# Block sums of the second channel weights: made by GpSimd, in other loop units, in a hybrid encoder layer

## The chip, the cores and the metric

The kernel runs on one core of one Trainium2 chip. The metric is device time in microseconds (us), the median of a few runs; lower is better. The core's engines are TensorE (PE, matmuls), VectorE (DVE), ScalarE (ACT), GpSimd (POOL) and SyncE (SP); before the change, every DMA is issued by SyncE.

## What is computed

One layer of a streaming encoder on x of 2048 tokens x 1024 channels, float32: a token mixer of four head groups (convolution, state-space scan, windowed attention, gated recurrence), and then the channel mixer, with which this case deals:

```python
h = rmsnorm(x, norm_ffn[l])
x = x + (jnp.square(jax.nn.relu(h @ w_ff1[l])) @ w_ff2[l]).astype(x.dtype)
```

w_ff1 is 1024 x 4096, w_ff2 4096 x 1024.

## The kernel before

The whole layer is one program. A scheduler turns the code into one fixed instruction order for each engine before the kernel runs: it goes by priorities (a block under `hi_()` has a high one), by data dependences and by the times that it assumes for every operation. Tiles come from pools; a tag has a fixed number of buffers, and whoever takes a buffer again waits for its last users. Each engine then works through its own order and waits where a semaphore has not come yet. SyncE too: a DMA that it cannot issue yet holds up all DMAs behind it.

Every float32 operand of a matmul is split into a rounded part and a rest (h and l, made by ScalarE and VectorE), and a product takes three passes: h.h, h.l, l.h.

**The channel mixer's products** are done by a scheme of seven block products instead of eight (Strassen's, in Winograd's form) at 2 x 2 blocks. It needs sums of blocks of both operands, and so there are four steps:

- `prep_step`: loads normed token rows (tile fxs), transposes them and makes the seven token operands. For the first token half they stay in SBUF; for the second they are stored to DRAM (tb) during units 2, 5, 8 and 11, and `from_dram` loads them again (tile tr, lines 1216 to 1218) when the second half begins.
- `ff1`: one unit makes 256 hidden channels for 1024 tokens: seven products of 12 matmuls (line 1267), relu and square on ScalarE (1273, 1274), block sums on VectorE (1138), and seven stores (as, line 1310). There are 16 units for each token half, 32 in all, here numbered 0 to 31 (n = 16 hf + j). ScalarE's copy at line 1286 stands once in each.
- `w_units`: loads four 128 x 512 blocks of w_ff1 for the next unit (a11, a12, a21, a22; tile wr, line 1134, six buffers), makes four sums on VectorE (the first adds a21 and a22) and splits seven operands (wh on ScalarE at line 1128, wl on VectorE at 1129).
- `w2_sums(k)`, k from 0 to 15: loads two rows of blocks of w_ff2, each 128 x 1024, 512 KB (x and y, tile w2r), forms four differences of 128 x 512 blocks in place, and stores both to DRAM (tt). The second phase of the mixer loads tt (`t_unit`) as the weight operand of four of its seven block products, after the units.

The second phase runs 7 x 8 groups of 48 matmuls (line 1397). Its token operands come back from DRAM through tile sr (`s_tile`, lines 1367 to 1369).

**What sets the order around the change.** fxs, tr, w2r and sr all take the tag xt, which has two buffers, in the order in which the code asks for them. Before the change that is: fxs of the fourth prep_step (unit 11), tr (14 loads), w2r (32 tiles, in units 16 to 31), sr. SyncE issues the loads and stores of w2_sums between the stores as and the loads wr of the units; VectorE makes the differences between the units' own sums.

Of the kernel before, what the change touches and what calls it, by code (L numbers as in the profile page):

```python
# [16 lines left out]
ALU = mybir.AluOpType  # L17
# [4 lines left out]
P = 128  # L22
# [37 lines left out]
def emit(ctx, tc, a):  # L60
    nc = tc.nc
    V, S, G, PE, SY = nc.vector, nc.scalar, nc.gpsimd, nc.tensor, nc.sync
# [104 lines left out]
    for r in range(2):  # L167
        SY.dma_start(out=sink[r * 64:(r + 1) * 64, :],
                     in_=a["attn_sinks"].rearrange("(k r) -> r k", r=2)[r].partition_broadcast(64),
# [945 lines left out]
    NJ = DFF // (2 * P)  # L1115
    as_d = [[dram.tile([P, 4, NJ, P], F32, name=f"as{i}_{h}") for h in range(2)] for i in range(7)]
    tt_d = [dram.tile([NJ, P, D], F32, name=f"tt{i}") for i in range(2)]
# [19 lines left out]
    def tsub(o, x, y, op=ALU.subtract):  # L1137
        V.tensor_tensor(out=o, in0=x, in1=y, op=op)  # L1138
# [15 lines left out]
    def prep_step(hf, i, put, tmp):  # L1154
        def trans(ps, xs, half):
            for k in range(4):
                kk = half * 4 + k
                PE.transpose(ps[:, k * P:(k + 1) * P], xs[:, kk * P:(kk + 1) * P], ident)

        o = i * P  # L1160
        xs = []
        for tb in range(2):
            x_ = big.tile([P, D], F32, tag="xt", name="fxs", bufs=2)
            SY.dma_start(out=x_, in_=x1_d[hf * 2 + tb][o:o + P, :])
            ss = c1.tile([P, 1], F32, tag="fss", name="fss", bufs=2)
            S.activation(out=junk, in_=x_, func=AF.Square, accum_out=ss)
            r = rstd_of(c1, ss, 1, 1.0 / D, "frs")
            V.scalar_tensor_tensor(out=x_, in0=x_, scalar=r, in1=g_ffn, op0=ALU.mult, op1=ALU.mult)
            xs.append(x_)
        p11, p22 = psum_tr(), psum_sx()  # L1170
        trans(p11, xs[0], 0)
        trans(p22, xs[1], 1)
        s11, s22 = tmp(), tmp()
        S.activation(out=s11, in_=p11, func=AF.Copy)
        S.activation(out=s22, in_=p22, func=AF.Copy)
        p12, p21 = psum_tr(), psum_sx()
        trans(p12, xs[1], 0)
        trans(p21, xs[0], 1)
        put(0, o, s11)
        put(1, o, p21)  # L1180
        t1, t2 = tmp(), tmp()
        tsub(t1, p12, s11)
        tsub(t2, s22, t1)
        t4 = tmp()
        tsub(t4, p21, t2)
        t3 = tmp()
        tsub(t3, s22, p12)
        put(2, o, t2)
        put(3, o, t1)
        put(4, o, t3)  # L1190
        put(5, o, s22)
        put(6, o, t4)
# [8 lines left out]
    def put_dram(tmp):  # L1201
        def put(i, o, src):
            if i == 1:
                c_ = tmp()
                S.activation(out=c_, in_=src, func=AF.Copy)
                src = c_
            SY.dma_start(out=tb_d[i][:, :, o:o + P], in_=src.rearrange("p (k t) -> p k t", k=4))
        return put

    def from_dram():  # L1210
        ops = operands()
        for i in range(7):
            for h in range(2):
                ks = slice(h * 2, h * 2 + 2)
                r = big.tile([P, 2, TB], F32, tag="xt", name="tr", bufs=2)
                SY.dma_start(out=r, in_=tb_d[i][:, ks, :])
                S.activation(out=ops[i][0][:, ks], in_=r, func=AF.Copy)
                V.tensor_tensor(out=ops[i][1][:, ks], in0=r, in1=ops[i][0][:, ks], op=ALU.subtract)
        return ops


    def w2_sums(k):
        x_, y_ = (big.tile([P, D], F32, tag="xt", name="w2r", bufs=2) for _ in range(2))
        for h, t_ in enumerate((x_, y_)):
            SY.dma_start(out=t_, in_=a["w_ff2"][(2 * k + h) * P:(2 * k + h + 1) * P, :])
        b11, b12, b21, b22 = x_[:, 0:512], x_[:, 512:], y_[:, 0:512], y_[:, 512:]
        tsub(b11, b12, b11)
        tsub(b12, b22, b12)
        tsub(b22, b22, b11)
        tsub(b21, b21, b22)  # L1230
        for h, t_ in enumerate((x_, y_)):
            SY.dma_start(out=tt_d[h][k], in_=t_)

    def w2(k, half, nd):
        return a["w_ff2"][(2 * k + half) * P:(2 * k + half + 1) * P, nd * 512:(nd + 1) * 512]
# [2 lines left out]
    def w_units(j, tmp):  # L1238
        f0 = j * 2 * P

        def raw(kh, fh):
            return raw512(a["w_ff1"][kh * 512:(kh + 1) * 512, f0 + fh * P:f0 + (fh + 1) * P]
                          .rearrange("(k p) c -> p k c", p=P))

        with hi_():
            a11, a12, a21, a22 = raw(0, 0), raw(1, 0), raw(0, 1), raw(1, 1)
            u = [split(a11), split(a12)]
            s1, s2 = tmp(), tmp()
            tsub(s1, a21, a22, ALU.add)
            tsub(s2, s1, a11)  # L1250
            u.append(split(s2))
            u.append(split(s1))
            s3, s4 = tmp(), tmp()
            tsub(s3, a11, a21)
            u.append(split(s3))
            tsub(s4, a12, s2)
            u.append(split(s4))
            u.append(split(a22))
        return u
# [16 lines left out]
    def ff1(hf, j, u, b, tmp):  # L1276
        pa, pb, pc = psum_mm(), psum_mx(), psum_hx()
        prod(pa, u[0], b[0], True)
        x1 = tmp()
        S.activation(out=x1, in_=pa, func=AF.Copy)  # L1280
        prod(pb, u[1], b[1], True)
        c11 = tmp()
        tsub(c11, pb, x1, ALU.add)
        prod(pa, u[2], b[2], False)
        u2 = tmp()
        S.activation(out=u2, in_=pa, func=AF.Copy)  # L1286
        relu2(c11, c11)
        prod(pc, u[3], b[3], True)
        p5 = tmp()
        S.activation(out=p5, in_=pc, func=AF.Copy)  # L1290
        prod(pa, u[4], b[4], False)
        c22 = tmp()
        tsub(c22, pa, p5, ALU.add)
        relu2(c22, c22)
        prod(pc, u[5], b[5], False)
        c12 = tmp()
        tsub(c12, pc, u2, ALU.add)
        relu2(c12, c12)
        prod(pa, u[6], b[6], False)
        c21 = tmp()  # L1300
        relu2(c21, pa)

        e11, e12, e21, e22 = c11, c21, c12, c22
        s1, s2, s3, s4 = tmp(), tmp(), tmp(), tmp()
        tsub(s1, e21, e22, ALU.add)
        tsub(s2, s1, e11)
        tsub(s3, e11, e21)
        tsub(s4, e12, s2)
        for i, t_ in enumerate((e11, e12, s2, s3, e22, s1, s4)):
            SY.dma_start(out=as_d[i][hf][:, :, j, :], in_=t_.rearrange("p (q t) -> p q t", q=4))  # L1310
# [9 lines left out]
    for hf in range(2):  # L1320
        for j in range(NJ):
            u = nxt
            if (hf, j) != (1, NJ - 1):
                nxt = w_units((j + 1) % NJ, tmp1)
            if hf == 0 and j in (2, 5, 8, 11):
                prep_step(1, (2, 5, 8, 11).index(j), put_dram(tmp1), tmp1)
            if hf == 1 and j == 0:
                with hi_():
                    b = from_dram()
            if hf == 1:  # L1330
                w2_sums(j)
            ff1(hf, j, u, b, tmp1)
    f2.close()

# [106 lines left out]
```

## Time and profile before

| what | value |
|---|---|
| median of 3 runs | 2346.17 us (2341.35 to 2346.51) |
| the profiled execution's own time | 2343.7 us |
| its span in the profile | 2341.6 us |
| TensorE matmul, busy | 2227.5 us (95%) |
| VectorE, busy | 1433.2 us (61%) |
| ScalarE, busy | 949.8 us (41%) |
| GpSimd, busy | 163.2 us (7%), 208 instructions |
| mean granted TensorE clock | 0.987 |

The span is the profiled execution from its first to its last instruction; its own time lies 2.1 us above. In the views, a row of the timeline is: start, duration, engine, line, operation, output <- inputs, shapes, count, and in brackets the engine's idle time ahead of it and what ended that. A row of waits is: engine, tile and line, what it waited for, total us, times, longest. A row of the table by stretch has the stretch, its length, then busy time and instruction count of each engine, the granted clock, the DMA engines' busy share and GB/s. A row of DMA issues gives the count, the size and the median time from issue to landing. PEld is TensorE's weight load.

### The profile page before, as it was taken

To read this page: it belongs to the slowest core of one execution; us is meant where nothing else is said; L and a number is where in the kernel's file an instruction comes from. 1 tells how busy PE (TensorE), PEld (TensorE's weight loads), DVE (VectorE), ACT (ScalarE), POOL (GpSimd) and SP (SyncE) were. 2 spreads that over 40 slices of the span, in tenths; PEclk is the share of its full clock that TensorE was granted. 3 is DMA by queue.
4 is the path that set the end of the run, shared out by engine and by line. 5 is a ranking of instruction groups with operands and counts; after the bars stand their busy time and mean duration, and the time that the engine had idled before them with its cause. 6 is when DMAs were issued, how large, how long until landed. Compare 5 with 4: busy or idle time off the path is not lost.

```text
span 2341.6 us, 32446 instructions
## 1 busy us (share of the span) xinstructions
PE 2227.5 (95%) x11460; PEld 1761.9 (75%) x11460; DVE 1433.2 (61%) x3008; ACT 949.8 (41%) x1902; POOL 163.2 (7%) x208
## 2 busy tenths in 40 slices
PE   7799999999999999989999999999999999999999
PEld 6577777777777777767777777777778888888887
DVE  5786786787677654676655666676653344344342
ACT  4234325435433433455555554544543233133121
POOL 0122212121211110000000000000000000000000
PEclk9899999999999999999999999999999999999999
DMA  6323333434432547636656577888674454355542
GB/s 182 92 78 97 104 102 118 118 101 125 124 111 85 163 155 224 216 129 193 194 158 191 173 222 255 273 266 267 204 238 151 155 192 140 118 190 180 183 148 99
DMA packets 393347, 381.35 MB, mean 163 GB/s; under 512 B 35968, under 2 KB 310496, under 8 KB 393184
## 3 DMA queue, kind: packets, MB, share of 16 engines
q1 hardware_dynamic: 393184, 379.27, 52.5%
q8 instruction: 90, 1.47, 0.3%
q14 instruction: 73, 0.60, 0.1%
HBM read 261.77 MB, written 116.40 MB: 161 GB/s over the span
## 4 chain that ended last, share of the span: by engine, by line
PE 67%; DVE 13%; DMA 9%; ACT 4%; issue 3%; POOL 2%; SPq 1%; DVEq 0%; POOLq 0%; ACTq 0%
PE mm L1397 26%; PE mm L1267 10%; PE mm L509 5%; PE mm L511 5%; PE mm L510 5%; PE hx L1267 5%; DMA w2r<-in_w_ff_dram 2%; DVE wl L111 2%; PE mx L1267 2%; DVE tp L1138 2%; PE hx L921 1%; DMA fxs<-x1d 1%; PE mx L826 1%; ACT wh L1128 1%; DVE w2r L1138 1%
## 5 line engine op out<-in xcount | busy, mean ns | idle before, releaser
L1397 PE MATMUL mm<-wh,st 128*128 128x512 f32 x1792 | 561.8, 394 | 1.4 <-ACT wh L1128 1.4
L1397 PEld LDWEIGHTS mm<-wh,st 128*128 128x128 f32 x1792 | 337.4, 188 | 80.0 <-ACT wh L1128 1.9
L1397 PE MATMUL mm<-wl,st 128*128 128x512 f32 x896 | 353.6, 395 | 0.2 <-DVE wl L1129 0.2
L1267 PE MATMUL mm<-tb,wh 128*128 128x512 f32 x1024 | 330.3, 403 | 24.5 <-ACT tp L1280 6.5
L1368 ACT ACTIVATE st<-sr 128x1024 fp32r<-128x1024 f32 x112 | 114.6, 1054 | 402.8 <-PE mm L1397 359.2
L1267 PEld LDWEIGHTS mm<-tb,wh 128*128 128x128 f32 x1024 | 189.6, 191 | 85.1 <-ACT tp L1286 14.7
L105 ACT ACTIVATE wh<-wr 128x512 fp32r<-128x512 f32 x224 | 138.6, 628 | 201.8 <-PE mm L510 163.0
L509 PE MATMUL mm<-wh,hh 128*128 128x512 f32 x512 | 208.3, 407 | 2.1 <-ACT hh L504 2.1
L1129 DVE TENSOR_TENSOR wl<-wr,wh 128x512 fp32r<-128x512 f32 x208 | 138.1, 688 | 113.6 <-ACT wh L1128 70.2
L1267 PE MATMUL mm<-tb,wl 128*128 128x512 f32 x512 | 204.5, 399 | 0.0
L511 PE MATMUL mm<-wh,hl 128*128 128x512 f32 x512 | 204.4, 399 | 0.0
L510 PE MATMUL mm<-wl,hh 128*128 128x512 f32 x512 | 204.0, 398 | 0.0
L1397 PEld LDWEIGHTS mm<-wl,st 128*128 128x128 f32 x896 | 168.4, 188 | 40.5 <-DVE wl L1129 0.5
L1369 DVE TENSOR_TENSOR st<-sr,st 128x1024 fp32r<-128x1024 f32 x112 | 133.9, 1222 | 94.8 <-ACT st L1368 94.6
L1267 PE MATMUL hx<-tb,wh 128*128 128x512 f32 x512 | 162.3, 397 | 8.4 <-ACT wh L1128 8.4
L111 DVE TENSOR_TENSOR wl<-wr,wh 128x512 fp32r<-128x512 f32 x224 | 151.3, 694 | 30.5 <-ACT wh L105 26.3
L509 PE MATMUL mm<-hh,wh 128*128 128x512 f32 x384 | 159.5, 415 | 0.0
L511 PE MATMUL mm<-hh,wl 128*128 128x512 f32 x384 | 154.9, 403 | 0.0
L510 PE MATMUL mm<-hl,wh 128*128 128x512 f32 x384 | 154.5, 402 | 0.0
L1128 ACT ACTIVATE wh<-wr 128x512 fp32r<-128x512 f32 x208 | 125.4, 625 | 64.6 <-PE mm L1267 28.1
L1138 DVE TENSOR_TENSOR tq<-mm,tq 128x512 f32<-128x512 f32 x32 | 22.1, 691 | 173.0 <-PE mm L1397 172.9
L1273 ACT ACTIVATE tp<-tp 128x512 f32<-128x512 f32 x96 | 60.5, 630 | 163.0 <-DVE tp L1138 156.2
(372 smaller groups left out, 3627.6 us busy)
## 6 DMA issues: line engine op xcount, KB each, us to landing
as<-tp SPq DMA_DIRECT2D x224, 256.0 KB, 2.8
sr<-as SPq DMA_DIRECT2D x112, 512.0 KB, 4.4
wr<-in_w_ff_dram SPq DMA_DIRECT2D x176, 256.0 KB, 3.8
wr<-in_w_in_dram SPq DMA_DIRECT2D x160, 256.0 KB, 3.1
wr<-in_w_out_dram SPq DMA_DIRECT2D x64, 256.0 KB, 4.1
w2r<-in_w_ff_dram SPq DMA_DIRECT2D x32, 512.0 KB, 4.6
tt<-w2r SPq DMA_DIRECT2D x32, 512.0 KB, 2.7
wr<-tt SPq DMA_DIRECT2D x64, 256.0 KB, 4.0
```

The source lines that it names most:

```text
L105: S.activation(out=hi, in_=raw, func=AF.Copy)
L111: (G if le == "p" else V).tensor_tensor(out=lo, in0=raw, in1=hi, op=ALU.subtract)
L509: PE.matmul(ps, lhsT=lh, rhs=rh, start=first, stop=False)
L510: PE.matmul(ps, lhsT=lh, rhs=rl, start=False, stop=False)
L511: PE.matmul(ps, lhsT=ll, rhs=rh, start=False, stop=last)
L1128: S.activation(out=h, in_=raw, func=AF.Copy)
L1129: V.tensor_tensor(out=l, in0=raw, in1=h, op=ALU.subtract)
L1138: V.tensor_tensor(out=o, in0=x, in1=y, op=op)
L1267: PE.matmul(ps, lhsT=(wh, wl)[lw][:, ks], rhs=b[lb][:, k, :], start=first and k == 0 and q == 0, stop=k == 3 and q == 2, skip_group_check= ...
L1368: S.activation(out=s_[:, 0, ks], in_=r, func=AF.Copy)
L1369: V.tensor_tensor(out=s_[:, 1, ks], in0=r, in1=s_[:, 0, ks], op=ALU.subtract)
L1397: PE.matmul(ps, lhsT=st_[:, ls, k, :], rhs=tu[i, k][lt], start=k == 0 and p_ == 0, stop=k == NJ - 1 and p_ == 2)
```

## The change

The loads, the four differences and the stores of `w2_sums` go to GpSimd (G), from SyncE (SY) and VectorE. And the calls stand in other units: k = 0 to 3 in units 12 to 15, k = 4 to 15 in units 18 to 29; before, k = 0 to 15 in units 16 to 31.

```diff
     def w2_sums(k):
         x_, y_ = (big.tile([P, D], F32, tag="xt", name="w2r", bufs=2) for _ in range(2))
         for h, t_ in enumerate((x_, y_)):
-            SY.dma_start(out=t_, in_=a["w_ff2"][(2 * k + h) * P:(2 * k + h + 1) * P, :])
+            G.dma_start(out=t_, in_=a["w_ff2"][(2 * k + h) * P:(2 * k + h + 1) * P, :])
         b11, b12, b21, b22 = x_[:, 0:512], x_[:, 512:], y_[:, 0:512], y_[:, 512:]
-        tsub(b11, b12, b11)
-        tsub(b12, b22, b12)
-        tsub(b22, b22, b11)
-        tsub(b21, b21, b22)
+        for o, p_, q_ in ((b11, b12, b11), (b12, b22, b12), (b22, b22, b11), (b21, b21, b22)):
+            G.tensor_tensor(out=o, in0=p_, in1=q_, op=ALU.subtract)
         for h, t_ in enumerate((x_, y_)):
-            SY.dma_start(out=tt_d[h][k], in_=t_)
+            G.dma_start(out=tt_d[h][k], in_=t_)
...
-            if hf == 1:
-                w2_sums(j)
+            n = hf * NJ + j
+            if 12 <= n < 16 or 18 <= n < 30:
+                w2_sums(n - 12 if n < 16 else n - 14)
             ff1(hf, j, u, b, tmp1)
```

The order of xt becomes: fxs of the fourth prep_step, w2r (8 tiles), tr, w2r (24 tiles), sr. Lines behind w2_sums have numbers one or two lower than before (as is L1308, sr L1366, the matmuls L1265).

On GpSimd, behind its last operation of before (frs, the norm of the fourth prep_step), the changed kernel has 16 groups like the two that follow; tt_10363 and tt_10364 are the two halves of tt.

```order
L93 TENSOR_TENSOR frs<-frs,mhalf 128x1 x16
L1225 DMA w2r<-in_w_ff_dram 128x1024 x2
L1228 TENSOR_TENSOR w2r<-w2r 128x512 x3
L1230 DMA tt_10363<-w2r 128x1024
L1228 TENSOR_TENSOR w2r<-w2r 128x512
L1230 DMA tt_10364<-w2r 128x1024
L1225 DMA w2r<-in_w_ff_dram 128x1024 x2
```

In before the frs row is followed only by the end of the program. The pair of loads of one call is behind both stores of the call before it.

On SyncE, before, the first reload of the second half's operands (tr from tb_10365) stands among the stores tb of the fourth prep_step:

```order
L1134 DMA wr<-in_w_ff_dram 128x4x128 x3
L1207 DMA tb_10365<-tp 512x1x128
L1207 DMA tb_10370<-tp 512x1x128
L1134 DMA wr<-in_w_ff_dram 128x4x128
L1207 DMA tb_10366<-tp 512x1x128
L1216 DMA tr<-tb_10365 128x1024 x2
L1207 DMA tb_10367<-tp 512x1x128
```

In the changed kernel it stands two units' stores later, with loads of the next weights between its two halves and behind them:

```order
L1308 DMA as_0_10353<-tp 512x1x128
L1308 DMA as_0_10355<-tp 512x1x128
L1308 DMA as_0_10361<-tp 512x1x128
L1216 DMA tr<-tb_10365 128x1024
L1134 DMA wr<-in_w_ff_dram 128x4x128
L1216 DMA tr<-tb_10365 128x1024
L1134 DMA wr<-in_w_ff_dram 128x4x128 x3
```

It waits there for the stores of call 3, by GpSimd.

On SyncE again, before, the first load sr of the second phase stands behind the last stores of w2_sums, in the stores of unit 28:

```order
L1225 DMA w2r<-in_w_ff_dram 128x1024
L1310 DMA as_1_10350<-tp 512x1x128
L1232 DMA tt_10363<-w2r 128x1024
L1232 DMA tt_10364<-w2r 128x1024
L1367 DMA sr<-as_0_10349 128x1024
L1310 DMA as_1_10358<-tp 512x1x128
L1367 DMA sr<-as_0_10349 128x1024
```

In the changed kernel it stands six units earlier, in the stores of unit 22 (as_1 is the second half's, 10350 the first of a unit's seven):

```order
L1308 DMA as_1_10350<-tp 512x1x128
L1308 DMA as_1_10358<-tp 512x1x128
L1308 DMA as_1_10360<-tp 512x1x128
L1366 DMA sr<-as_0_10349 128x1024
L1308 DMA as_1_10352<-tp 512x1x128
L1366 DMA sr<-as_0_10349 128x1024
L1134 DMA wr<-in_w_ff_dram 128x4x128 x3
```

It waits there for the stores of call 15, and the loads wr of the next weights are behind it.

## The prediction

> **What bounds the kernel now.** I read the page first, then busy time by stretch, TensorE's waits in the stretch where the touched work runs, and the spacing of the FFN units.
>
> ```profile
> span 2341.6 us, 32446 instructions
> ...
> PE 67%; DVE 13%; DMA 9%; ACT 4%; issue 3%; POOL 2%; SPq 1%; DVEq 0%; POOLq 0%; ACTq 0%
> ```
>
> The chain that ends last is TensorE for two thirds. The next two answers are the table by stretch and TensorE's waits from 1395 to 1660 us, where all 16 calls of w2_sums run.
>
> ```profile
> core 0: us, PE busy (x) PEld busy (x) DVE busy (x) ACT busy (x) POOL busy (x), PEclk, DMA share, GB/s
> 1300.00:1330.00 30.00, 30.00 (x131) 23.86 (x130) 15.81 (x25) 15.77 (x28) 0.00 (x0) 1.00 0.39 115
> 1395.00:1480.00 85.00, 79.12 (x322) 59.95 (x322) 57.79 (x92) 40.41 (x71) 0.00 (x0) 0.98 0.84 263
> 1480.00:1560.00 80.00, 75.98 (x316) 58.74 (x315) 57.33 (x91) 37.95 (x67) 0.00 (x0) 0.98 0.83 265
> 1560.00:1660.00 100.00, 96.04 (x403) 74.55 (x403) 67.13 (x107) 48.32 (x84) 0.00 (x0) 1.00 0.82 259
> ```
>
> ```profile
> PE hx L1267 <- ACT wh L1128: 7.4, 5, 2.3
> PE hx L1267 <- DVE wl L1129: 3.4, 8, 0.5
> PE mm L1267 <- ACT tp L1273: 2.1, 2, 1.2
> PE mm L1267 <- DVE tp L1138: 0.9, 2, 0.7
> ```
>
> Without that work (1300 to 1330) TensorE never idles and GpSimd does nothing. With it, TensorE idles 5.88 + 4.02 + 3.96 = 13.9 us in 265, almost all on ScalarE and VectorE making the next unit's weight halves. One ScalarE copy, L1286, comes once in a unit and is my clock; the rows are its first, second and third clean unit, then units 16 and 17, then the last two (31 is the last).
>
> ```profile
> 1280.78 0.58 ACT L1286 ACTIVATE tp<-mm 128x512 f32<-128x512 f32 x1
> 1300.14 0.58 ACT L1286 ACTIVATE tp<-mm 128x512 f32<-128x512 f32 x1
> 1319.70 0.58 ACT L1286 ACTIVATE tp<-mm 128x512 f32<-128x512 f32 x1
> ...
> 1387.99 0.58 ACT L1286 ACTIVATE tp<-mm 128x512 f32<-128x512 f32 x1
> 1412.15 0.58 ACT L1286 ACTIVATE tp<-mm 128x512 f32<-128x512 f32 x1
> ...
> 1686.86 0.58 ACT L1286 ACTIVATE tp<-mm 128x512 f32<-128x512 f32 x1
> 1702.30 0.58 ACT L1286 ACTIVATE tp<-mm 128x512 f32<-128x512 f32 x1
> ```
>
> A clean unit is 19.4 to 19.6 us, here 19.5. The 15 steps from unit 16 to unit 31 took 1702.30 - 1387.99 = 314.3 us.
>
> **What is removed.** 64 subtractions leave VectorE and 64 DMA issues leave SyncE.
>
> ```profile
> L1138 DVE TENSOR_TENSOR w2r<-w2r x64: 680/691/694, 1399.8 to 1653.7; 128x512 f32<-128x512 f32 x64
> L1225 SPq DMA_DIRECT2D w2r<-in_w_ff_dram x32: 328/376/627, 1395.1 to 1644.5; - x32
> L1232 SPq DMA_DIRECT2D tt<-w2r x32: 326/330/1088, 1404.8 to 1654.4; - x32
> ...
> wr<-in_w_ff_dram SPq DMA_DIRECT2D x176, 256.0 KB, 3.8
> w2r<-in_w_ff_dram SPq DMA_DIRECT2D x32, 512.0 KB, 4.6
> tt<-w2r SPq DMA_DIRECT2D x32, 512.0 KB, 2.7
> ```
>
> That is 64 x 0.691 = 44 us of VectorE, most of it beside TensorE. What it is worth is the stretched units: clean, the 15 steps would be 22 us for the first (it still ends the reload of the second half's operands; my estimate between 19.5 and the 24.2 seen) plus 14 x 19.5, and 3.4 us for the two stretches with a clock of 0.98 (each 0.02 of 80 to 85 us, 1.7), which I let stand: 298.4. Gain 314.3 - 298.4 = **15.9 us**. The 13.9 us of idle time above is the same thing read another way, the low end; 15 x 19.5 without the 22 and the 3.4 would give 21.8, the high end.
>
> **What is added: one round on GpSimd.** A round is one call of w2_sums. Both xt buffers serve every round, so rounds cannot overlap: y's load can start only when y's last store has landed, then three subtractions need y, with x's store issued between them, then y's store. The trace of before has no DMA from GpSimd. Its nearest subtraction-like rows are these, a group of 128x512 operations, and neighbours on GpSimd and VectorE in an earlier stage:
>
> ```profile
> L904 POOL TENSOR_TENSOR hacc<-ident,he 128x512 f32<-128x512 f32 x16 | 18.2, 1160 | 84.5 <-DVE he L900 57.4 <-DVE carry L648 25.0 <-DVE bp L941 2.0
> ```
>
> ```profile
> 390.32 1.67 POOL L939 TENSOR_TENSOR KQ<-KQ,bp 128x256 f32<-128x256 f32 x1
> ...
> 779.54 0.62 POOL L939 TENSOR_TENSOR KQ<-KQ,bp 128x256 f32<-128x256 f32 x1 [6.48 <-PE hx L924]
> 780.12 0.73 POOL L980 TENSOR_TENSOR hg<-hg,ogain 128x256 f32<-128x256 f32 x1
> ```
>
> ```profile
> 390.23 1.28 DVE L487 SCALAR_TENSOR_TENSOR xt<-xt,rsx,g_mix 128x1024 f32<-128x1024 f32 x1 [0.73 <-POOL rsx L93]
> ...
> 778.64 0.67 DVE L111 TENSOR_TENSOR wl<-wr,wh 128x512 fp32r<-128x512 f32 x1
> 780.22 1.18 DVE L111 TENSOR_TENSOR wl<-wr,wh 128x512 fp32r<-128x512 f32 x1 [0.25 <-ACT wh L105]
> ```
>
> The two engines hold each other up. VectorE's subtraction of two SBUF tiles took 0.67 us alone and 1.18 when it began under GpSimd's at 780.12; GpSimd's multiply took 0.62 alone and 1.67 beside VectorE's long operation at 390.23.
>
> So a subtraction costs 1.16 us, up to 1.16 + 0.69 when it first waits for a VectorE operation; I add 0.3. An issue by GpSimd is bounded by SyncE's shortest and longest of these transfers, 0.33 and 1.09; I take 1.0, near the upper, because here the engine that computes also issues. A landing is 4.6 for a load and 2.7 for a store, to which I add 0.7 each, the part of the 1.0 that SyncE's 0.33 does not hold already. The round is (4.6 + 0.7) + 3 x 1.46 + 1.0 + (2.7 + 0.7) = **14.1 us**. Lower end: 4.6 + 3 x 1.16 + 0.33 + 2.7 = 11.1. Upper end: (4.6 + 1.1) + 3 x 1.85 + 1.1 + (2.7 + 1.1) = 16.2.
>
> [...] No run here shows a DMA from GpSimd.
>
> **What is moved: two waits on SyncE.** GpSimd's queue holds nothing else (the last of its frs operations come with the fourth prep_step), so rounds follow back to back from the moment xt is free, wherever the loop emits them. SyncE's order was fixed beforehand, and the loads that reuse xt now wait there for GpSimd's stores: tr after round 3, sr after round 15. Behind both stand the wr loads of the next weights, and for them VectorE, ScalarE and then TensorE.
>
> ```profile
> 1274.40 0.60 PE L1158 MATMUL sx<-ident,fxs 128*128 128x128 f32 x4
> ...
> 1308.67 2.66 DVE L1138 TENSOR_TENSOR tp<-tp 128x512 f32<-128x512 f32 x4 [1.36 <-ACT tp L1274]
> ...
> 1313.36 3.92 SPq L1134 DMA_DIRECT2D wr<-in_w_ff_dram  x4
> ...
> 1316.19 0.68 DVE L1129 TENSOR_TENSOR wl<-wr,wh 128x512 fp32r<-128x512 f32 x1
> ...
> 1330.82 0.69 DVE L1138 TENSOR_TENSOR tp<-wr 128x512 f32<-128x512 f32 x1
> ...
> 1397.54 1.23 DVE L1218 TENSOR_TENSOR tb<-tr,tb 128x1024 fp32r<-128x1024 f32 x1 [1.89 <-ACT tb L1217]
> ```
>
> *First wait.* xt is free at 1274.40 + 0.60 = 1275.0. Loading x first costs 1.0, four rounds end at 1276.0 + 4 x 14.1 = 1332.4. Then SyncE issues tr (0.4, as the median w2r above) and the wr load behind it (0.5, between that row's 0.376 and 0.627), which lands 3.8 later: 1337.1. In before that wr was issued in the group at 1313.36 and first used at 1330.82, where VectorE adds a21 and a22; so there were some 13 us to spare, and they are used up. In the clean unit around it TensorE keeps pace with these halves, so what VectorE is late, TensorE is late: 1337.1 - 1330.8 = **6.3 us**, 0 at a round of 11.1, 14.7 at 16.2.
>
> *Second wait.* Round 4 starts when the last tr has been split, 1397.54 + 1.23 = 1398.8. Twelve rounds end at 1398.8 + 169.2 = 1568.0, and with sr (0.4), two wr issues (1.0) and a landing (3.8) the weights are there at 1573.2. SyncE's new order puts sr in unit 22. On the clean clock that unit's L1286 comes at 1388.0 + 22 + 5 x 19.5 = 1507.5, and the same addition follows a unit's L1286 by 1330.82 - 1300.14 = 30.7: the weights are wanted at 1538.2. TensorE stands for 1573.2 - 1538.2 = **35.0 us**; for a round of R us that is 12 R - 134.2, so 0 at 11.1 and 60.2 at 16.2. The result stores (as) behind sr hold tp buffers, which could stop it earlier; I have no row for that and leave it out. Both stalls move the later clock alike, so they add.
>
> *Interference.* VectorE's chain from the tail of one unit to the weights of the next (1308.67 to 1316.19 + 0.68 in the clean unit, 8.2 of 19.4 us or 42%) must not be late. Of the 16 subtractions in the first four rounds about 7 fall into it, at 1.18 - 0.67 = 0.5 each: 3.5 us at most, of which I take **2**, since a wait absorbs some. In the twelve later rounds it lies inside the 35 us.
>
> **Sum.** 35.0 + 6.3 + 2 - 15.9 = **+27.4 us**. The profiled execution took 2343.7 us and would take 2371.1; the median of the runs, 2346.17, is 2.5 higher, so 2373.6, rounded to **2374**. The break-even round is 12.3 us: 12 x 12.34 - 134.2 + 2 - 15.9 = 0, the first wait being nothing there.
>
> **The rivals.**
>
> *GpSimd is quick enough.* Rounds of about 11 us, the lower end: neither wait on SyncE holds anything up. What is left is the gain of 15.9 against interference: 42% of 64 operations, 27 hits at 0.5 us, 13.5 us, of which slack in the chain takes half. That is -9.1: **2337**. For it: the 4.6 us landing was measured on busy DMA queues (share 0.83) and could shorten. Against it: two waits of 1.0 are then free. Chance 0.14; it decides below 12.3 us a round.
>
> *Nothing to measure.* The same, with the slack gone: -15.9 + 13.5 = -2.4, **2344**. Also here: the rounds fall near break-even. Chance 0.11.
>
> *The shared path alone.* No wait on SyncE matters, but every hit holds VectorE for all of GpSimd's operation: 27 x 1.16 = 31, less 15.9: +15, **2361**. For it: 780.22 ended only after GpSimd had. Against: 0.5 is what it lost, not 0.73. Chance 0.1. [...]
>
> *GpSimd is slower still.* Rounds of 16.2: 60.2 + 14.7 + 2 - 15.9 = +61, **2407**. Chance 0.1.
>
> **How the numbers follow.** The forecast has the rest, 0.55, with rounds of 12.7 to 15.6 us and so 2351 to 2397. A measurement of this kernel can tell about 0.3%, 7 us, from no change. Slower by more: 0.55 + 0.1 + 0.1 = 0.75. Within: 0.11. Faster: 0.14. The range takes in the rivals down to 2337 and up to just under the slowest, 2405, and leaves out the outer half of both.
>
> **What would show it.** Right: GpSimd's stores tt 14 us apart; SyncE idle for tens of microseconds ahead of the first sr; a wait of TensorE of about 35 us in units 22 to 24 and one of some 6 us in units 13 to 15; units 26 to 30 at 19.5. Wrong: rounds below 12 us, or SyncE held ahead of sr without TensorE stopping, which would mean that the weights have more to spare than 13 us.

## The result, and the profile after

| what | before | after |
|---|---|---|
| median | 2346.34 us (2341.35 to 2348.4, 4 runs) | 2378.41 us (2375.88 to 2384.54, 4 runs) |
| ratio to before | 1 | 1.0138 (95%: 1.0111 to 1.0166) |
| the profiled execution's own time | 2343.7 us | 2375.88 us |
| span, mean granted clock | 2341.6 us, 0.987 | 2374.1 us, 0.981 |

Slower by 32 us; 2374 (2337 to 2405) was forecast. First the page: the chain that ended last has less TensorE and more DMA and GpSimd in it, and GpSimd's DMAs (POOLq, with the median time from issue to landing) are there.

```profile
PE 64%; DMA 13%; DVE 9%; issue 5%; POOL 5%; ACT 3%; SPq 0%; POOLq 0%; DVEq 0%; ACTq 0%
...
w2r<-in_w_ff_dram POOLq DMA_DIRECT2D x32, 512.0 KB, 5.1
tt<-w2r POOLq DMA_DIRECT2D x32, 512.0 KB, 3.4
```

Next the instructions on tile w2r, with durations (min/median/max, ns), then GpSimd's timeline: the store of y ends a round, and the rows are the ends of rounds 0 and 3, the first load of round 4, and the ends of rounds 4 and 15.

```profile
L1228 POOL TENSOR_TENSOR w2r<-w2r x64: 1255/1299/1807, 1274.7 to 1579.0; 128x512 f32<-128x512 f32 x64
L1225 POOL DMA_DIRECT2D w2r<-in_w_ff_dram x32: 542/542/767, 1267.5 to 1570.9; - x32
L1230 POOL DMA_DIRECT2D tt<-w2r x32: 579/582/584, 1278.9 to 1580.6; - x32
```

```profile
1281.08 0.58 POOL L1230 DMA_DIRECT2D tt<-w2r  x1 [0.30 <-POOL w2r L1228]
...
1324.43 0.58 POOL L1230 DMA_DIRECT2D tt<-w2r  x1 [0.30 <-POOL w2r L1228]
1403.10 0.54 POOL L1225 DMA_DIRECT2D w2r<-in_w_ff_dram  x1 [78.08 <-DMA tr<-tb]
...
1417.13 0.58 POOL L1230 DMA_DIRECT2D tt<-w2r  x1 [0.30 <-POOL w2r L1228]
...
1580.60 0.58 POOL L1230 DMA_DIRECT2D tt<-w2r  x1 [0.30 <-POOL w2r L1228]
```

A round took (1324.43 - 1281.08) / 3 = 14.45 us in the first half and (1580.60 - 1417.13) / 11 = 14.86 in the second. Between them GpSimd waited 78 us for the xt buffers that tr held. SyncE's own timeline shows both of its waits.

```profile
1293.20 13.79 SPq L1308 DMA_DIRECT2D as<-tp  x7
1325.30 0.34 SPq L1216 DMA_DIRECT2D tr<-tb  x1
...
1535.46 10.39 SPq L1308 DMA_DIRECT2D as<-tp  x3
1581.49 0.34 SPq L1366 DMA_DIRECT2D sr<-as  x1
...
1584.55 1.49 SPq L1134 DMA_DIRECT2D wr<-in_w_ff_dram  x3
```

SyncE stood 18.3 us ahead of tr and 1581.49 - 1535.46 - 10.39 = 35.6 ahead of sr. TensorE's longest wait from 1510 to 1600 us, and ScalarE's copy that stands once in a unit (here units 12, 13, 14, 16, 22, 23, 24, 31):

```profile
PE mm L1265 <- ACT tp L1271: 16.3, 1, 16.3
```

```profile
1293.83 0.58 ACT L1284 ACTIVATE tp<-mm 128x512 f32<-128x512 f32 x1
1318.95 0.58 ACT L1284 ACTIVATE tp<-mm 128x512 f32<-128x512 f32 x1
1348.97 0.58 ACT L1284 ACTIVATE tp<-mm 128x512 f32<-128x512 f32 x1
...
1396.15 0.58 ACT L1284 ACTIVATE tp<-mm 128x512 f32<-128x512 f32 x1
...
1536.08 0.58 ACT L1284 ACTIVATE tp<-mm 128x512 f32<-128x512 f32 x1
1561.27 0.58 ACT L1284 ACTIVATE tp<-mm 128x512 f32<-128x512 f32 x1
1600.66 0.58 ACT L1284 ACTIVATE tp<-mm 128x512 f32<-128x512 f32 x1
...
1734.39 0.58 ACT L1284 ACTIVATE tp<-mm 128x512 f32<-128x512 f32 x1
```

The steps from unit 12 to 31 took 1734.39 - 1293.83 = 440.6 us; in before they took 1702.30 - 1300.14 = 402.2. That is +38.4; unit 12 came 6.3 us earlier here, ahead of everything that the change touches but the first rounds, and after unit 31 the two differ by 0.4. The long stop lies in the step from unit 23 to 24: 39.4 us. But the seven steps ahead of it, from unit 16, took 1561.27 - 1396.15 = 165.1 us, 23.6 each, so much was lost with no long stop in sight. That is what the experiments had to explain. One table by stretch says a third thing, the granted clock (PEclk, third number from the end): before, then after.

```profile
1200.00:1760.00 560.00, 526.60 (x2202) 409.14 (x2201) 358.96 (x547) 287.50 (x486) 1.10 (x2) 0.99 0.74 229
```

```profile
1200.00:1760.00 560.00, 500.05 (x2048) 389.97 (x2046) 329.92 (x457) 274.01 (x463) 125.61 (x130) 0.95 0.70 215
```

### The profile page after: what moved, and what is told of

Its sections match the earlier page's. It is cut to its first block, busy times and chain, and to the rows that moved or that the text cites. A ratio compares the mean times of both kernels' runs of the same rounds, so it can differ in the third digit from the quotient of the medians.

```text
span 2374.1 us, 32463 instructions
## 1 busy us (share of the span) xinstructions
PE 2232.6 (94%) x11460; PEld 1767.6 (74%) x11460; DVE 1423.4 (60%) x2944; ACT 952.2 (40%) x1902; POOL 288.5 (12%) x336
## 4 chain that ended last, share of the span: by engine, by line
PE 64%; DMA 13%; DVE 9%; issue 5%; POOL 5%; ACT 3%; SPq 0%; POOLq 0%; DVEq 0%; ACTq 0%
PE mm L1396 25%; PE mm L1265 8%; PE mm L509 5%; PE mm L511 5%; PE mm L510 5%; DMA w2r<-in_w_ff_dram 4%; PE hx L1265 3%; POOL w2r L1228 3%; DMA tt<-w2r 2%; DVE wl L111 2%; PE mx L1265 2%; PE hx L921 1%; DMA fxs<-x1d 1%; PE mx L826 1%; DMA xt<-in_x_dram 1%
## 5 line engine op out<-in xcount | busy, mean ns | idle before, releaser
L1265 PE MATMUL mm<-tb,wh 128*128 128x512 f32 x1024 | 336.8, 410 | 38.4 <-ACT tp L1271 18.3
L1265 PEld LDWEIGHTS mm<-tb,wh 128*128 128x128 f32 x1024 | 195.0, 196 | 98.5 <-ACT tp L1271 24.1
L1265 PE MATMUL mm<-tb,wl 128*128 128x512 f32 x512 | 207.3, 405 | 0.0
L1265 PE MATMUL hx<-tb,wh 128*128 128x512 f32 x512 | 164.1, 401 | 6.5 <-ACT wh L1128 6.4
L111 DVE TENSOR_TENSOR wl<-wr,wh 128x512 fp32r<-128x512 f32 x224 | 151.4, 694 | 30.3 <-ACT wh L105 24.1
L1271 ACT ACTIVATE tp<-tp 128x512 f32<-128x512 f32 x96 | 60.5, 631 | 164.8 <-DVE tp L1138 157.9
```

Source lines behind the costliest of these rows:

```text
L111: (G if le == "p" else V).tensor_tensor(out=lo, in0=raw, in1=hi, op=ALU.subtract)
L1265: PE.matmul(ps, lhsT=(wh, wl)[lw][:, ks], rhs=b[lb][:, k, :], start=first and k == 0 and q == 0, stop=k == 3 and q == 2, skip_group_check= ...
```

## The experiments

The theory on record with the forecast: SyncE's two waits (the queue theory). Its main rival: GpSimd and VectorE lengthen each other's work (the shared path), which costs without any wait of SyncE.

### What the sums cost in before, and what is left without SyncE's waits

**e3_no_sums** takes the sums out of before:

```diff
-            if hf == 1:
-                w2_sums(j)
...
-            return split2(raw512(tt_d[h][k][:, n * 512:(n + 1) * 512]))
+            return split2(raw512(w2(k, h, n)))
```

> The kernel before without the block sums: it leaves out all 16 calls of w2_sums, and the second phase reads blocks of w_ff2 where it read the sums. Both theories take the same bound for what the sums cost before: the prediction's 15.9 us, so 2330. If it is 2338 or more, the gain in the sum was too large; below 2324, too small.

Measured: 2322.87 us (2318.99 to 2330.05), ratio 0.9914 (0.9884 to 0.9945). All that the sums cost in before is 22 us, more than the 15.9 forecast; the second phase, which reads blocks of w_ff2 in their place, takes as long (from unit 31's copy to the end 638.2 us, in before 639.3). Its rows for units 12, 16, 17, 29 and 31 are the yardstick for the rest:

```profile
1301.34 0.58 ACT L1286 ACTIVATE tp<-mm 128x512 f32<-128x512 f32 x1
...
1387.96 0.58 ACT L1286 ACTIVATE tp<-mm 128x512 f32<-128x512 f32 x1
1410.99 0.58 ACT L1286 ACTIVATE tp<-mm 128x512 f32<-128x512 f32 x1
...
1645.79 0.58 ACT L1286 ACTIVATE tp<-mm 128x512 f32<-128x512 f32 x1
...
1680.79 0.58 ACT L1286 ACTIVATE tp<-mm 128x512 f32<-128x512 f32 x1
```

From unit 17 on every unit takes (1645.79 - 1410.99) / 12 = 19.57 us, and units 12 to 31 take 379.5: before is 22.7 above it, after 61.1.

**e1_own_buffers** gives the rounds of the changed kernel buffers of their own, so that neither tr nor sr waits for them:

```diff
-        x_, y_ = (big.tile([P, D], F32, tag="xt", name="w2r", bufs=2) for _ in range(2))
+        x_ = c1.tile([P, D], F32, tag="gain", name="w2x")
+        b21, b22 = (c1.tile([P, 512], F32, tag="xr", name="w2y", bufs=2) for _ in range(2))
```

> The changed kernel with buffers of its own for the block sums (x in the buffer of the norm gains, y in the two of the mixer's residual tile, both free in this stage), so that neither tr nor sr waits for GpSimd; the work on GpSimd is the same. Queue theory (the prediction: SyncE's two waits cost 35 and 6 us, interference little): both waits gone, interference half absorbed, 2337, at most 2345. Rival, the shared path: units 17 to 22 of the changed kernel took 20.2 to 26.2 us beside GpSimd's rounds instead of 19.5; if that stretch of some 3.7 us a unit comes with the rounds and not with the waits, 16 rounds of 14.5 us cover some 11 or 12 units and cost about 40 us, against 15.9 gained: 2365 to 2372.

Measured: 2367.02 us (2363.98 to 2374.04), ratio 1.0095 (1.0065 to 1.0125). This is where the shared path stands, not the queue theory: 11 of the 32 us go, 22 stay. It is no clean subtraction, since the rounds moved too: nothing holds them now; they run back to back beside units 8 to 17, and there TensorE loses the time. By the copy that stands once in a unit, in the profiled execution (2374.04 us, the longest of the four), units 18 to 30 take 19.57 us each, but units 8 to 18 take 1483.3 - 1217.1 = 266.2 us, and without sums 1430.6 - 1216.8 = 213.8: 52 us more for 16 rounds.

**e10_late_second_wait** leaves the changed kernel as it is, but ScalarE first copies a column of unit 27 into the two buffers of sr:

```diff
+            if n == 27:
+                with hi_():
+                    xt = [big.tile([P, 8, P], F32, tag="xt", name="sr", bufs=2) for _ in range(2)]
+                    for r in xt:
+                        S.activation(out=r[:, 0, 0:1], in_=u2[:, 0:1], func=AF.Copy)
```

> The changed kernel, but the first two loads of the second phase take their buffers only after ScalarE has copied a column from unit 27 into them, so that SyncE does not reach them before the rounds are over; everything else stands. Theory that the second wait of SyncE costs its TensorE stop of 16.3 us and half of the 17 us of half clock behind it: 2352 to 2364. The prediction's own size of that wait, 35 us: 2340 to 2348. Rival, that the rounds themselves cost it and the wait only shows it: 2368 to 2380.

Measured: 2381.43 us (2367.34 to 2391.1), ratio 1.0156 (1.0113 to 1.0199): no gain as a whole, a little above even the rival's range, and not for the rival's reason. The buffers now go to sr ahead of the last two rounds, and so the wait came back later: GpSimd made those rounds from 1726 to 1756 us, the second phase's next loads waited for them, and TensorE stopped there.

```profile
PE mm L1402 <- ACT st L1373: 18.7, 1, 18.7
```

What the trial does give is the price of the wait where it had stood. Its units 18, 23 and 24:

```profile
1446.80 0.58 ACT L1284 ACTIVATE tp<-mm 128x512 f32<-128x512 f32 x1
...
1564.41 0.58 ACT L1284 ACTIVATE tp<-mm 128x512 f32<-128x512 f32 x1
1583.98 0.58 ACT L1284 ACTIVATE tp<-mm 128x512 f32<-128x512 f32 x1
```

The step from unit 23 to 24 is 19.57 again, 19.8 less than in after. The steps ahead of it stay long (117.6 from unit 18 to 23, in after 117.1): these are not the wait's doing.

### Who moves, who subtracts, and where

Three kernels complete a square with the changed one, all with its places and its shared buffers. e4_places_only is before with only the places changed; e2_vector_subtracts is the changed kernel with `tsub` on VectorE; e8_sync_moves_gpsimd_subtracts is the changed kernel with the loads and stores on SyncE:

```diff
# e4, on before
-            if hf == 1:
-                w2_sums(j)
+            n = hf * NJ + j
+            if 12 <= n < 16 or 18 <= n < 30:
+                w2_sums(n - 12 if n < 16 else n - 14)
# e2, on after
-            G.tensor_tensor(out=o, in0=p_, in1=q_, op=ALU.subtract)
+            V.tensor_tensor(out=o, in0=p_, in1=q_, op=ALU.subtract)
# e8, on after (the stores likewise)
-            G.dma_start(out=t_, in_=a["w_ff2"][(2 * k + h) * P:(2 * k + h + 1) * P, :])
+            SY.dma_start(out=t_, in_=a["w_ff2"][(2 * k + h) * P:(2 * k + h + 1) * P, :])
```

> The kernel before with the new places alone: SyncE and VectorE do the block sums in units 12 to 15 and 18 to 29. No GpSimd, so the rounds are as in before and SyncE's order of tr and sr is made with its own loads and stores around them. Queue theory: no long wait, within 5 us of before, 2341 to 2351. Shared path: the same. A loss of over 10 us would say that the places themselves cost, through tr standing behind four rounds of xt.

> The changed kernel with the four subtractions back on VectorE; loads and stores stay with GpSimd, in the same units and in the same buffers. No subtraction on GpSimd, so nothing shared. Rounds of about 14.7 - 3 x (1.30 - 0.69) - 0.6 = 12.3 us. Queue theory: SyncE still waits ahead of tr and sr for GpSimd's stores, shorter by 12 x 2.4 = 29 us at sr, so 6 to 10 us of stall are left, and VectorE's 44 us are back in the units: 2343 to 2353. Shared path: nothing of the loss is left, and SyncE has 64 issues less: 2335 to 2346.

> The changed kernel with the loads and stores of the rounds on SyncE's queue again and only the subtractions on GpSimd, same places and buffers as the change. It completes a square: SyncE moves and VectorE subtracts at these places took 2360.9, GpSimd moves and VectorE subtracts 2380.1, GpSimd does both 2378.4. Theory that GpSimd's subtractions lengthen VectorE's work: 2372 to 2390, since SyncE now also stands for the subtractions (1.3 us each in place of 0.69). Rival, that what costs is that GpSimd moves the data: 2358 to 2366, as with VectorE's subtractions.

| moved by | VectorE subtracts | GpSimd subtracts |
|---|---|---|
| SyncE | e4: 2360.93, ratio 1.006 (1.0034 to 1.0086) | e8: 2363.05, ratio 1.0077 (1.005 to 1.0104) |
| GpSimd | e2: 2380.1, ratio 1.0154 (1.0125 to 1.0182) | after: 2378.41, ratio 1.0138 (1.0111 to 1.0166) |

The places alone cost 16 us, which no theory had expected. The profiled execution of e4 took 2350.67 us, 7 more than that of before, so its trace holds less than half of it. There the four rounds beside units 12 to 15 cost most: units 11 to 15 took 95.6 us, without sums 84.1, so 2.9 a round, and the 12 later rounds (308.1 - 292.8) / 12 = 1.3 each. The rest stays open. Both theories missed e2 too, and e8 came where its rival, the transfers, had it: with shared buffers it matters who moves the data (15 to 19 us), and not who subtracts (2 us either way). The rows show who waited for tile w2r in e4, then in e2 (us, times):

```profile
  DVE w2r L1138: 38.7, 20
```

```profile
  DVE w2r L1228: 58.7, 24
```

When VectorE subtracts, its own order stands still until the load is there, and behind a load of GpSimd it stood 20 us longer, about the difference. So e2 exchanged one loss for another, and the square doesn't separate the shared path from the transfers. The next four do.

### Subtractions alone, transfers alone, both

All four have e1's own buffers. A round is held until ScalarE has written its copy of the unit before, so that one round lies beside one unit (12 to 15, 18 to 29); in e5 and e7 this holds only the tile of x. e5_paced_all is whole; e6 leaves out the transfers of the rounds and e7 the subtractions; e9 is e7 with all three tiles held. In e6, e7 and e9 the second phase reads blocks of w_ff2, as in e3.

```diff
# e5, in w2_sums
+        G.tensor_tensor(out=x_[:, 0:1], in0=pace[:, 0:1], in1=pace[:, 0:1], op=ALU.subtract)
# e6: loads for round 0 alone, no stores
+        if k == 0:
...
-        for h, t_ in enumerate((x_, y_)):
-            G.dma_start(out=tt_d[h][k], in_=t_)
# e7 and e9
-        for o, p_, q_ in ((b11, b12, b11), (b12, b22, b12), (b22, b22, b11), (b21, b21, b22)):
-            G.tensor_tensor(out=o, in0=p_, in1=q_, op=ALU.subtract)
# e9
+        for t_ in (x_, b21, b22):
+            G.tensor_tensor(out=t_[:, 0:1], in0=pace[:, 0:1], in1=pace[:, 0:1], op=ALU.subtract)
```

> Own buffers for the rounds as in the run before with own buffers, and each of the 16 rounds on GpSimd first reads one column of the tile that ScalarE wrote in the unit before, so that at most one round goes beside a unit (units 12 to 15 and 18 to 29) and none runs ahead. Loads, subtractions and stores are GpSimd's. SyncE waits for no buffer of the rounds. The run with own buffers and rounds back to back took 2367.0 and the one without sums 2322.9, 44 us for 16 rounds, 2.8 a round. Theory that a round costs the same wherever it lies (VectorE and GpSimd lengthen each other's work): 2360 to 2372 again. Rival, that it was the crowding of eleven rounds beside the reloads of the operands in units 9 to 18 that cost so much: 2335 to 2350, since only four rounds lie there now.

> As the paced kernel, but GpSimd loads its two buffers once and then only subtracts in them, four subtractions for each of the 16 rounds; the loads and stores of the rounds are left out and the second phase reads the weights themselves instead of the sums. Theory that the subtractions on GpSimd and those on VectorE lengthen each other: most of the paced kernel's excess over the run without sums (2322.9) stays, 2340 to 2362. Rival, that the transfers cost it: 2321 to 2330.

> As the paced kernel, but the 64 subtractions are left out: GpSimd issues the loads and the stores of each round and nothing else, and the second phase reads the weights themselves. Theory that the subtractions lengthen VectorE's work: 2321 to 2332, near the run without sums (2322.9). Rival, that the transfers (32 MB in all beside the weights' loads) cost it: 2340 to 2362. If both this and the run with subtractions alone lie halfway, the cost is shared.

> The run with transfers only once more, with both halves of a round held by the reading of the unit before (there only the first half was; the second half ran far ahead, beside units 0 to 4, and stopped TensorE 21.3 us). The subtractions are left out and the second phase reads the weights themselves. With one half paced (512 KB in and 512 KB out a unit) units 17 to 29 took 19.57 us each, as without sums. Theory that what costs is the amount that GpSimd moves beside a unit, 1 MB in and 1 MB out: 2338 to 2358, with units 18 to 28 at 20.5 to 21.5 us as in the paced kernel. Rival, that transfers and subtractions cost only together (the subtractions lengthen VectorE's work just when the weights are late): 2322 to 2332, and units at 19.6 us.

| kernel | us | ratio to before | units 18 to 28, us each |
|---|---|---|---|
| e3, no sums | 2322.87 | 0.9914 (0.9884 to 0.9945) | 19.6 |
| e6, subtractions only | 2323.26 | 0.9913 (0.9889 to 0.9938) | 19.6 |
| e9, transfers only | 2324.05 | 0.9913 (0.9886 to 0.9941) | 19.6 |
| e5, both | 2356.5 | 1.0057 (1.0029 to 1.0086) | 20.9 to 21.6 |

e7 came to 2351.94, ratio 1.0025 (1.0002 to 1.0048), for a reason of its own (the half of its transfers that nothing held crowded beside units 0 to 4, where TensorE stopped once for 21.3 us; from unit 17 on its units took 19.57 us), and is set aside. The others are plain, and a surprise: 64 subtractions on GpSimd cost nothing, 32 MB moved by GpSimd cost nothing, and both together cost 33 us. e5 itself lies between its two ranges (2360 to 2372 and 2335 to 2350), so neither theory had its size. What differs is *when* in a unit the subtractions run. VectorE's timeline beside GpSimd's, for one unit of e6, in order of time within each engine:

```profile
1476.08 1.73 DVE L1129 TENSOR_TENSOR wl<-wr,wh 128x512 fp32r<-128x512 f32 x1 [2.98 <-PE mm L1271]
...
1480.96 2.62 DVE L1138 TENSOR_TENSOR tp<-tp 128x512 f32<-128x512 f32 x4 [1.49 <-ACT tp L1278]
```

```profile
1473.24 1.29 POOL L1236 TENSOR_TENSOR w2x<-w2x 128x512 f32<-128x512 f32 x1
...
1477.34 1.63 POOL L1236 TENSOR_TENSOR w2y<-w2y 128x512 f32<-128x512 f32 x1
```

From the hidden sums (tp<-tp at 1480.96) through the next unit's block sums to five of its seven weight halves VectorE works without a gap, and TensorE waits for what comes out of it. Ahead of that chain VectorE has gaps. In e6 GpSimd is done by 1479.0: only one subtraction of VectorE grew (1.73 us at 1476.08, others 0.69), and a gap took it up. With transfers in the round, GpSimd must wait for the load, and its subtractions slide onto the chain. One line by shape from 1420 to 1580 us (busy us, mean ns of one) shows it, for e6, then for e5:

```profile
L1138 DVE TENSOR_TENSOR tp<-tp 128x512 f32<-128x512 f32 x34 | 22.1, 688 | 13.7 <-ACT tp L1278 13.4
```

```profile
L1138 DVE TENSOR_TENSOR tp<-tp 128x512 f32<-128x512 f32 x30 | 33.5, 1153 | 11.2 <-ACT tp L1276 10.9
```

Four of them a unit, 0.465 us longer each, make 1.9 us; a unit of e5 is 1.3 to 2.0 us longer. But e5 differs in one more thing: only x was held there, its loads of y ran beside SyncE's loads of the next weights, and wr landed in 5.9 us (median from 1400 to 1580 us; e9 3.6, before 3.9). Which of the two costs the time, the next section tells.

### Putting the rounds where they should cost nothing

**e11_spread_halves** makes half a round (256 columns) beside each of the 32 units, **e12_between_weight_loads** 13 full rounds beside units 17 to 29 and 6 half rounds beside units without a preparation step; each starts behind its own unit's copy.

```diff
# e11
+            mark = ff1(hf, j, u, b, tmp1)
+            w2_sums(n, mark)
# e12
+            if n in (3, 4, 6, 7, 9, 10):
+                i = (3, 4, 6, 7, 9, 10).index(n)
+                w2_half(i // 2, i % 2 * 256, mark)
+            elif 17 <= n < 30:
+                w2_sums(n - 14, mark)
```

> GpSimd makes the sums in half rounds, 256 columns of each block, one beside each of the 32 units, in two own buffers, each held by a reading of one column of the unit's tile: 512 KB in and 512 KB out a unit, four subtractions of 128x256. Theory that 1 MB a unit is free and subtractions on GpSimd are free: 2322 to 2334, below both kernels. Rival, that the sums cost in proportion to their bytes whoever makes them and wherever: 2345 to 2358.

> GpSimd makes all the sums with its own loads and stores in buffers of its own, but each round starts when ScalarE has written the third product's copy of its unit, some 13 us before SyncE issues the next four loads of first weights: 13 full rounds beside units 17 to 29, and three rounds in halves (256 columns of each block) beside units 3, 4, 6, 7, 9 and 10, away from the units with a preparation step and from the reloads of the operands. Theory that the rounds cost only where their transfers run beside the loads of the first weights, the preparation or the reloads: 2322 to 2334, below both kernels. Rival, that subtractions and transfers of a full round in one unit lengthen each other whenever they are: units 17 to 29 at 20.5 to 21.5 us as in the paced kernel, 2340 to 2356.

e11 took 2349.2 us (2336.67 to 2357.45), ratio 1.0012 (0.9989 to 1.0034): no difference from before, in the range of its rival, though not for the rival's reason. Beside units 17 to 29 a half round is free, as the rows of units 17 and 28 show, (1653.08 - 1437.84) / 11 = 19.57; what it costs, it costs beside units with a preparation step or the reload of tr (unit 2 to 3: 27.8 us, without sums 21.2).

```profile
1437.84 0.58 ACT L1288 ACTIVATE tp<-mm 128x512 f32<-128x512 f32 x1
...
1653.08 0.58 ACT L1288 ACTIVATE tp<-mm 128x512 f32<-128x512 f32 x1
```

e12 took 2370.66 us (2361.01 to 2379.78), ratio 1.0085 (1.0055 to 1.0115): above both of its ranges. My theory of that moment, that rounds cost only beside the loads of the weights, the preparation or the reloads, is wrong. The loads were out of the way (wr landed in 3.9 us, as in before), and a unit from 17 to 29 took (1697.01 - 1414.26) / 12 = 23.6 us:

```profile
1414.26 0.58 ACT L1305 ACTIVATE tp<-mm 128x512 f32<-128x512 f32 x1
...
1697.01 0.58 ACT L1305 ACTIVATE tp<-mm 128x512 f32<-128x512 f32 x1
```

One unit of it, VectorE and then GpSimd, is the clearest picture of the cause:

```profile
1491.98 0.69 DVE L1138 TENSOR_TENSOR tp<-hx,tp 128x512 f32<-128x512 f32 x1 [1.40 <-PE hx L1286]
1494.03 5.70 DVE L1138 TENSOR_TENSOR tp<-tp 128x512 f32<-128x512 f32 x4 [1.36 <-ACT tp L1293]
```

```profile
1491.52 1.30 POOL L1224 TENSOR_TENSOR w2x<-w2x 128x512 f32<-128x512 f32 x1 [3.21 <-DMA w2x<-in_w_ff_dram]
...
1493.72 1.30 POOL L1224 TENSOR_TENSOR w2x<-w2y,w2x 128x512 f32<-128x512 f32 x1
1495.10 1.64 POOL L1224 TENSOR_TENSOR w2y<-w2y,w2x 128x512 f32<-128x512 f32 x1
...
1497.27 1.31 POOL L1224 TENSOR_TENSOR w2y<-w2y 128x512 f32<-128x512 f32 x1
```

Three of GpSimd's four subtractions fall on VectorE's four sums: 5.70 us in place of 2.62 (e6), while GpSimd's own take 1.30 to 1.64. The one at 1491.98, which reads hx from PSUM, kept its 0.69 beside GpSimd's at 1491.52. From 1420 to 1580 us the 28 sums of this kind took 1.40 us each on the mean, and every other kind of operation on VectorE its 0.68 to 0.69. After shows the same side by side: in these 160 us the kinds of operation on VectorE whose inputs all lie in SBUF took 0.78 to 1.30 us on the mean (in e3 0.68 to 0.69), and those that read a PSUM tile (mm, hx or mx) still 0.68 to 0.69. Why that is so, no run shows.

So the theory that stands: a round of GpSimd costs by the part of its subtractions that falls on VectorE's gapless chain, and SyncE's waits come on top. One gap is left: no run put the subtractions on the chain without their transfers. That the transfers have no share of their own in e12 rests on e9, where rounds of the same transfers ran free beside units 18 to 29; and for e5 the late wr and the longer sums were not told apart. Half rounds in units 17 to 29 fit it: in a unit of e11 GpSimd's last subtraction ended at 1485.44, and VectorE's chain began at 1485.52. There is no room there for all 32, and no version that beats before came out of this. Without the sums 22 us are to be had; e6 and e9 show that neither part must cost anything, and a round with its loads a unit ahead of its subtractions, which might join the two, wasn't tried.

## Why the prediction was right

The time was right within 5 us, with the right sign, and in part by luck. From unit 12 to 31 the change cost 38.4 us, 11 more than the sum of 27.4; 6.3 us came back ahead of unit 12, and 4.6 of these ahead of unit 0 (1037.21 against 1041.81), where nothing of the change runs. Inside the sum the second wait was 15 us too high, the interference some 32 too low and the gain 6 too low. By its own steps, with the yardstick of e3:

| step | predicted | measured |
|---|---|---|
| gain, units 16 to 31 | 15.9 (to 21.8) | 314.3 - 292.8 = 21.5 |
| a round | 14.1 | 14.45 and 14.86 |
| first wait | 6.3 | SyncE 18.3; step 13 to 14 30.0 in after, 24.1 in e3: 5.9, interference in it |
| second wait | 35.0 | SyncE 35.6; step 23 to 24 39.4 - 19.57 = 19.8, TensorE's stop 16.3 |
| interference, first half | 2 | units 12 to 16: 102.3 - 86.6 = 15.7, less the first wait's 5.9: 9.8 |
| interference, second half | "inside the 35 us" | units 16 to 23: 165.1 - 140.4 = 24.7, ahead of the wait |
| sum | +27.4 | 5.9 + 19.8 + 9.8 + 24.7 + 0.9 - 22.7 = +38.4 |

(In the sum, 0.9 is what remains after unit 24, and 22.7 is the gain from unit 12 on. The medians differ by 32, as do the profiled executions, where unit 12 came 6.3 us earlier.)

- **Gain.** The mechanism was right; but the 3.4 us of clock that "I let stand" went too, and the last step, from unit 30 to 31, takes 15.4 us and not the 19.5 of a clean unit, as the prediction's own last rows had shown. The high end was the value, by luck: its 15 equal steps leave out the long first and the short last. And of the 13.9 us of idle time, 3.0 were waits for tp and not for weight halves.
- **The round.** Right, from errors in its terms that cancel nearly: a subtraction took 1.30 where 1.46 had been taken, an issue 0.54 to 0.58 in place of 1.0, a load landed in 5.1 (5.3 taken), a store in 3.4 (3.4 taken). These give 13.0; the rest lies between them, as the 0.30 us ahead of each store of y, and wasn't taken apart.
- **The first wait.** The path was right: VectorE waited 3.56 us at 1334.03 for the loads wr. The step grew by 5.9 for 6.3, with interference in it. TensorE stopped three times for 2.4 us, and not once for 6.
- **The second wait** is the step that failed, in its clock and in its path. The clock: "On the clean clock that unit's L1286 comes at 1507.5". It came at 1536.08, 28.6 us later, as the units beside the rounds had been stretched. The loads came only 16 later: SyncE issued them at 1584.55, and with 0.5 for an issue and 3.9 to land they were there at 1589, against 1573.2. With the prediction's own 30.7 us the weights were wanted at 1566.8: 22 us late, near the 19.8 of the step. SyncE's own wait, 35.6, is near 35.0 by chance, since 35.0 was to be TensorE's loss. After unit 22's copy SyncE came to sr in 9.8 us; by the prediction's clock it would have been there at 1517 and have stood until 1568, some 51 us (an estimate).

The path: "The result stores (as) behind sr hold tp buffers, which could stop it earlier; I have no row for that and leave it out." They did. TensorE's 16.3 us ended on ScalarE's L1271, and that had waited for a store as; VectorE's wait for wr was short and came after it:

```profile
1587.04 0.60 ACT L1271 ACTIVATE tp<-mm 128x512 f32<-128x512 f32 x1 [17.25 <-DMA as<-tp]
...
1590.54 0.69 DVE L1138 TENSOR_TENSOR tp<-wr 128x512 f32<-128x512 f32 x1 [1.51 <-DMA wr<-in_w_ff_dram]
```

VectorE's last sum before the stop ended at 1571.85; with buffers free it would have wanted wr at about 1572.5 (an estimate), 18 us ahead of the loads. So the path that was forecast would have cost nearly as much, but it isn't the one that stopped TensorE.

- **"Both stalls move the later clock alike, so they add"**, and the interference of the later rounds "lies inside the 35 us". It is the other way round: it comes first, and the wait shrinks by what has been lost already. VectorE's chain was named rightly, but a hit was priced too low, at 0.5 us, and the lower clock that came with the waits (0.94 from units 16 to 23 in after, 1.00 in e3) had no term at all (the last section has its size). In after one unit shows what a full hit costs, three sums of 0.69 us at 1.73, 1.77 and 1.91, so 1.0 to 1.2 more each, near the 1.16 of the shared-path rival; the first of them:

```profile
1502.25 1.73 DVE L1138 TENSOR_TENSOR tp<-tp,wr 128x512 f32<-128x512 f32 x1
```

- **The rivals.** "The shared path alone" was put at 2361 with a chance of 0.1; e1, which has no wait of SyncE on the rounds, took 2367. By the table it was no rival but the larger half of the cause (9.8 and 24.7 us), and the waits the smaller (5.9 and 19.8). "GpSimd is quick enough" needed rounds below 12.3 us; none came near.
- **What would show it.** The stores 14 us apart, SyncE's idle time and units 26 to 30 at 19.57 came as written; TensorE's 35 us in units 22 to 24 were 16.3, and a single wait of some 6 in units 13 to 15 didn't come (the longest there was 2.9).

## What to carry to other kernels

When work moves to GpSimd, ask first at what moment of the loop its operations run: the same subtractions cost nothing in VectorE's gaps (e6) and 4 us a unit on VectorE's gapless chain (e12), half of it by the lower clock that came with the waits (an estimate), and a load ahead of them can push them from the one to the other. When two delays act on one chain, work the second out from the clock that the first has already moved; they don't simply add. And taking away a buffer wait by reordering may only send it elsewhere: follow who takes the buffer next (e10). And ask of everything that stands behind a stopped queue what it holds: here stores that kept their buffers stopped TensorE before the missing loads did.

## What was not expected of the hardware

- **The clock.** TensorE's granted clock from 1200 to 1760 us was 1.00 without sums, 0.99 in before and 0.95 in after, and 0.88 from 1525 to 1610, around the long stop. Its size, from units 16 to 23, after and then e3:

```profile
1396.20:1561.30 165.10, 149.00 (x596) 115.31 (x595) 105.80 (x130) 77.28 (x133) 81.48 (x83) 0.94 0.80 251
```

```profile
1396.20:1561.30 165.10, 164.61 (x706) 130.77 (x706) 97.44 (x154) 87.75 (x151) 0.00 (x0) 1.00 0.53 154
```

A matmul took 250 ns in after and 233 in e3, which for seven units of 84 is 10 us; TensorE's waits there add up to 16.1. The two together are near the 24.7 us of the table (estimates, since the profile models the ends of matmuls). In e12 it is half and half: from 1430 to 1730 us TensorE stopped 13 times for at most 2.1 us and 13 times for at most 0.5, 26.8 us in all, some 24.7 of the 48 that 12 units took longer, and the rest is longer matmuls (estimates), at a granted clock of 0.95 from 1400 to 1760 us. The waits were short: in the two units of e12 from 1453 to 1500 us TensorE stopped for 1.50 and 1.29 us and soon after for 0.50, and pairs of matmuls behind took some 1.05 us in place of 0.63; in three units of e5 (1457 to 1503 us), with 0.94, 0.41 and 0.71 and then 0.5, the pairs behind took 0.62 to 0.63. In after, where TensorE stopped for 16.3 us until 1587.7, the granted clock was 1.00 from 1571.4 to 1574, 0.50 from 1576 to 1592 and 1.00 again from 1593, and the pairs of matmuls in between took 1.05 us. No run changes the clock alone, and none shows what sets it.

- **GpSimd's DMAs** were issued in 0.54 to 0.58 us and landed in 5.1 and 3.4 us (medians, in after), where SyncE's of the same size in before took 0.33 to 0.38 and 4.6 and 2.7. The loads and stores of 16 rounds beside the units cost nothing by themselves (e9 took 2324.05 us, without sums e3 2322.87).
